# A hybrid decoder step on one core: norm factors fetched as rows from DRAM, gate products as 64x64 corners, the last token half in blocks of 228 and 114, schedule constants set anew

## The chip, the core and the metric

The kernel runs on one core of a Trainium2 chip. The metric is the device time of one execution in microseconds (us). The program is recorded through a tile layer: the code names instructions, tiles and priorities, a scheduler orders each engine's instructions once, at build time, and the chip then executes every engine's list strictly in that order, waiting on semaphores. An engine whose next instruction is not ready stands still even if a later one could run. All transfers named below are issued by SP (SyncE) or ACT, also in the order of their lists.

## What is computed

One decoder layer over 2048 prompt tokens and 8 sample tokens (2056 columns), D_MODEL 1024, all in fp32:

```python
xn = _rmsnorm(x, norm1_g)
z = jnp.einsum('btd,de->bte', xn, w_in)              # 1024 -> 1792
xr, gr, q, k, v = jnp.split(z, IN_SPLITS, axis=-1)
xc, new_conv = _causal_conv(xr, conv_buf, conv_w, conv_b)
# gates of the recurrence: 8 diagonal blocks of 64x64
r = jax.nn.sigmoid(_block_diag(xc, gate_a_w, gate_a_b))
i = jax.nn.sigmoid(_block_diag(xc, gate_x_w, gate_x_b))
...                                                   # linear recurrence -> rec
att = _prompt_attention(q, k, v, attn_sinks)          # window of 128, 8 heads
mix = jnp.concatenate([_rmsnorm(rec, rec_norm_g), _rmsnorm(att, attn_norm_g)], axis=-1)
h = x + jnp.einsum('bte,ed->btd', mix, w_out)
hn = _rmsnorm(h, norm2_g)
ff = jax.nn.silu(hn @ w_gate) * (hn @ w_up)           # 1024 -> 2816
y = h + ff @ w_down                                   # 2816 -> 1024
y_prompt = _rmsnorm(y, final_norm_g)
```

An RMSNorm multiplies each token by a factor of its own, rsqrt(mean(x²) + eps).

## The kernel before, in words

Channels lie on the 128 partitions, tokens on the free axis. Most products are split products: an operand is held as a rounded part `hi` and a remainder `lo` of type fp32r, and one product is three matmuls (hi·hi, hi·lo, lo·hi; lines L281 to L283, L1231 to L1233, L1268 to L1270, L1295 to L1297). The gate products (L608), the broadcasts (L319, L347), the sums (L304) and the transposes (L789) are plain fp32.

**First half (attention, recurrence, projections).** The tokens go in four parts s = 0 to 3 of 520, 512, 512 and 512 columns. For each part 14 units `ip` of 128 output channels each are computed (24 matmuls of 512 columns), then 8 units `op` of the output projection. A unit's weights come through a pool of five tiles; parts s > 0 fetch split weights that part 0 left in DRAM (`split_weights`, L262). The attention of part s (scores `s`, transposes `pt`, outputs `o`) and the recurrence of part s are threaded between the `ip` and `op` units of PE's list. `rec_chunk` computes the gates of 128 channels c: two 128x128 weights, each with two 64x64 blocks on the diagonal and zeros elsewhere, give two matmuls over the part's columns (four for part 0, whose 520 columns go in two halves of 260). Their results go to `m_tile`, a pool with a single PSUM bank, which the sums, the broadcasts and the transposes of V use as well; ACT reads each with a tanh (L610).

**A norm factor** is made as a column: PE sums squares over the partitions (`rstd_cols`, L304, one matmul for 86 to 128 tokens), DVE adds eps (L308), POOL takes the power −0.5 (L309). The factors of w tokens then lie on w partitions, and to multiply they must lie along the free axis on all 128. `row_bcast` (L319) does this with one fp32 matmul for each w tokens, column times identity, into `m_tile`, and ACT copies it to SBUF (L325). `half_bcast` (L347) does the same for the second norm, whose columns are kept in `rs2`.

**Second half (FFN).** The tokens go in three groups gi of two halves n (2x344, 2x342, 2x342 columns). 11 pairs p of 256 hidden channels are computed for each group: `ps_g` and `ps_u` (gate and up) and then the down product, which adds into `y`. Pairs 1 to 9 of gi = 1 and 2 use seven combined products in the place of eight (`pw`); the others use plain down products `pd`. Weights are split again for each group by ACT (hi), and by DVE or POOL (lo); tables `E_...` say for each such operation whether DVE ('V') or POOL ('P') does it.

**The end.** The last pair of gi = 2 goes half by half, n = 1 first. `finish` squares each `y` (ACT), adds the squares (POOL for n = 1, DVE for n = 0), forms the factors, and multiplies all 16 tiles (L1323, DVE), each followed by its store. Both halves are multiplied after the last product.

**What sets the order.** Each step is a generator that yields a planned time; instructions get the priority of that time, less a lead (`ahead`, the constants `L_...`, `F_...`). The scheduler takes the ready instruction with the first priority on each engine. So tables such as `T_IP`, `T_OP`, `T_ATT` and `ORDERS` decide how units, attention and recurrence lie between each other on PE, and on every other engine.

Of the kernel before, what the change touches and what calls it, by code (L numbers as in the profile page):

```python
# [12 lines left out]
P = 128  # L13
# [26 lines left out]
U_IP, U_OP = 6.19, 5.41  # L40
# [6 lines left out]
T_IP = [19.97, 89.2513, 240.41, 360.55]  # L47
T_OP = [187.9747, 327.9525, 449.0, 499.41]
T_OPA, L_LM = 524.66, 40.7
# [5 lines left out]
F_LEAD = [8.63, 18.27, 9.0, 1.0, 3.05, 1.57, 4.0, 2.24, 4.14]  # L55
F_HN = [26.25, 18.3, 31.9]
F_FIN = [13.89, 1.77, 6.51, 4.8]
F_MIX = [15.0, 62.67, 18.34, 64.97]
F_DOWN = [16.55, 11.4]
E_SUM = ['P', 'P', 'P', 'P']  # L60
E_LO0 = ['P', 'V', 'P', 'V', 'P', 'V', 'P']
E_LO1 = ['P', 'V', 'P']
E_LO2 = ['V', 'V', 'V']
E_DLO1 = ['P', 'V', 'P', 'V', 'V', 'P', 'V']
E_DLO2 = ['P', 'P', 'P', 'P', 'P', 'P', 'V']
E_DSUM = ['P', 'P', 'P', 'P', 'P', 'V', 'P', 'P']
E_T1 = ['P', 'P', 'P', 'V']
E_T2 = ['V', 'P', 'P', 'P']
E_HN = ['P', 'P', 'P', 'P']
E_MUL = ['P', 'V', 'V', 'P']  # L70

# [33 lines left out]
ORDERS = [[1, 12, 9, 8, 0, 3, 11, 10, 13, 2, 5, 4, 6, 7], [8, 9, 10, 11, 4, 0, 12, 13, 1, 5, 2, 6, 3, 7], [4, 0, 5, 1, 8, 12, 9, 10, 11, 2, 13, 7, 3, 6], [8, 12, 10, 9, 11, 13, 0, 4, 1, 6, 5, 2, 3, 7]]  # L105
T_ATT = [[-5.16, 6.82], [94.7626, 9.19], [318.03, 12.77], [454.6511, 8.38]]
T_MIX0 = 400.09
T_MIX = [None, T_B[0] + F_MIX[0], T_B[1] + F_MIX[2]]
T_REC = 46.56
L_PE, L_EV, L_DMA, L_W, L_PREP, D_PREP, L_AN, T_HN, D_HN, D_MIX = 195.07, 6.8, 44.07, 6.54, 16.82, -0.58, 33.49, 477.25, 7.78, 0.2  # L110
# [3 lines left out]
L_SW = 10.68  # L114
T_CACHE, T_LD, T_PRO = 126.26, 3.73, -37.62
D_REC = [10.95, 7.47]
D_ATT = [4.5, 3.07, 9.75, 5.73]
T_DVE = -4.47
T_DEC = 102.0
T_RN = [128.93, 254.29, 363.658, 427.88]  # L120
# [70 lines left out]
def hybrid_step(tc, xT, xR, vecs, cst, gatew, win, wout, wgate, wup, wdown, kT, vC, ck, cv, sconv, sh0,  # L191
                yT, pkT, pvT, pconv, phs, skw, svw, sconv_o, sh_o):
# [3 lines left out]
    with ExitStack() as ctx:  # L196
# [28 lines left out]

        def m_tile(name):
            return ps_m.tile([P, 512], F32, tag="m", name=name)
# [16 lines left out]
        mixed = dp.tile([3, 7, P, 4, TP], F32, name="mixed")  # L244
        split_s = {x: dp.tile([NPAIR, 4, P, 2, 512], F32, name=f"split_{x}") for x in "gu"}
# [5 lines left out]
        keep = tc.keep_in_program_order  # L251

# [25 lines left out]
        def mm3(out, ws, k, xh, xl, first, last):  # L278
            w, m0 = ws[k // 4], k % 4 * P
            wh, wl = w[:, 0, m0:m0 + P], w[:, 1, m0:m0 + P]  # L280
            nc.tensor.matmul(out, wh, xh, start=first, stop=False)  # L281
            nc.tensor.matmul(out, wh, xl, start=False, stop=False)  # L282
            nc.tensor.matmul(out, wl, xh, start=False, stop=last)  # L283
# [16 lines left out]
        def rstd_cols(acc, w, nt, which, out, name, lead=None, pin=False):  # L300
            ps = m_tile(f"st_{name}")
            with ahead(lead):
                for j in range(nt):
                    r = nc.tensor.matmul(ps[:w, j:j + 1], acc[:, j * w:(j + 1) * w], avg[:, which:which + 1],  # L304
                                         start=True, stop=True)
                    if pin and j == 0:
                        keep(r)
# [3 lines left out]
        def row_bcast(cols, w, nt, name, lead=None, keep_ps=False, pin=False):  # L311
            out = None if keep_ps else bcp.tile([P, TM], F32, tag="bc", name=f"rb_{name}")
            per = 512 // w
            for j0 in range(0, nt, per):
                jn = min(per, nt - j0)
                ps = (acc_tile if keep_ps else m_tile)(f"bc_{name}_{j0}")
                with ahead(lead):
                    for j in range(jn):
                        r = nc.tensor.matmul(ps[:, j * w:(j + 1) * w], cols[:, j0 + j:j0 + j + 1].to_broadcast([w, P]),  # L319
# [5 lines left out]
                nc.scalar.copy(out[:, j0 * w:(j0 + jn) * w], ps[:, :jn * w])  # L325
            return out
# [7 lines left out]
        def half_bcast(gi, n, name):  # L334
            o, nn = HALVES[gi][n]
            out = hbp.tile([P, TP], F32, tag="hb", name=f"hb_{name}")
            ps = m_tile(f"hb_{name}")
            for s, (c0, T, _, w, nt) in enumerate(SUBS):
                a, b = max(o, c0), min(o + nn, c0 + T)
                if a >= b:  # L340
                    continue
                j0, j1 = (a - c0) // w, (b - c0 - 1) // w + 1
                with ahead():
                    for j in range(j0, j1):
                        x, y = max(a, c0 + j * w), min(b, c0 + j * w + w)
                        d0 = x - c0 - j * w
# [1118 lines left out]
```

## Time and profile before

| | us |
|---|---|
| runs of the kernel | 2075.49, 2079.70, 2086.09 (median 2079.7) |
| profiled execution, its time | 2083.33 |
| its span, first to last instruction | 2081.6 |
| PE busy with matmuls | 2020.7 (97%) |
| DVE / ACT / POOL busy | 1438.9 / 937.7 / 935.7 |
| mean share of 16 DMA engines, queue q1 | 62.8% |

A row of a group has the line, the engine, the operation, the tiles written and read, and the count; then busy time, mean ns of one, and the idle time of the engine just before with the instruction that ended it. Matmuls overlap, so the pace of PE is read from start to start in the timeline, not from durations. One fp32 matmul that isn't a transpose shows as two records.

### The profile page before, as it was taken

Reading aid. Unit: us, or ns where it says so; the run is one execution under the profiler, and the core shown is the slowest. Engines: PE = TensorE matmul, PEld = TensorE weight load, DVE = VectorE, ACT = ScalarE, POOL = GpSimd, SP = SyncE. Lnnn points to the kernel's source line nnn. Section 1 sums busy time; section 2 is a strip of 40 time slices with the busy share of each in tenths; the row PEclk is TensorE's granted clock in tenths of the full one; section 3 lists DMA queues with packets and bytes.
Section 4 is the critical chain, followed back from the end, with each engine's and each line's share of the span. In section 5 each row is a group of like instructions: output and inputs, shape, how many; then the busy total and the mean of one; then the engine's idle time right before and its main releaser. Section 6 shows DMA issues by size and latency. Waiting matters only on the chain.

```text
span 2081.6 us, 34706 instructions
## 1 busy us (share of the span) xinstructions
PE 2020.7 (97%) x12238; PEld 1910.1 (92%) x12238; DVE 1438.9 (69%) x2683; ACT 937.7 (45%) x1954; POOL 935.7 (45%) x820
## 2 busy tenths in 40 slices
PE   8999899999999899999999999999999999999997
PEld 8988787878877799999999999999999999999997
DVE  6786885766986655656654568777776667777676
ACT  5774684553564453334334533333334533333342
POOL 5211342030123688767775845445546622332332
PEclk9999999999999899999999999999999999999998
DMA  8764485575677855556555776767677675556652
GB/s 299 258 212 155 156 290 172 186 239 191 212 265 267 290 215 195 213 194 226 197 188 178 269 263 203 246 232 236 204 249 252 235 232 197 195 189 195 196 181 94
DMA packets 208989, 450.95 MB, mean 217 GB/s; under 512 B 25232, under 2 KB 82720, under 8 KB 208800
## 3 DMA queue, kind: packets, MB, share of 16 engines
q1 hardware_dynamic: 205616, 446.24, 62.8%
q10 hardware_dynamic: 3200, 2.51, 0.4%
q8 instruction: 96, 1.57, 0.3%
q14 instruction: 77, 0.63, 0.1%
HBM read 335.89 MB, written 113.84 MB: 216 GB/s over the span
## 4 chain that ended last, share of the span: by engine, by line
PE 51%; DMA 4%; DVE 4%; POOL 3%; issue 3%; ACT 1%; SPq 0%; DVEq 0%; POOLq 0%; ACTq 0%
PE ps_u L1231 6%; PE ps_u L1232 6%; PE ps_u L1233 6%; PE ps_g L1231 5%; PE ps_g L1232 5%; PE ps_g L1233 5%; PE pw L1296 3%; PE pw L1295 3%; PE pw L1297 3%; PE pd L1268 3%; PE pd L1269 3%; PE pd L1270 3%; DMA n<-hs 2%; DVE y L1323 1%; DMA rd<-in_wdown 1%
## 5 line engine op out<-in xcount | busy, mean ns | idle before, releaser
L1231 PE MATMUL ps_g<-hn,w_g 128*128 128x342 f32 (+1 forms) x924 | 296.6, 321 | 5.5 <-DVE xres L942 2.6
L1231 PE MATMUL ps_u<-hn,w_u 128*128 128x342 f32 (+1 forms) x924 | 297.0, 321 | 1.4 <-ACT c_u L1241 0.8
L1232 PE MATMUL ps_g<-hn,w_g 128*128 128x342 f32 (+1 forms) x924 | 296.0, 320 | 2.4 <-DVE hn L433 2.4
L1232 PE MATMUL ps_u<-hn,w_u 128*128 128x342 f32 (+1 forms) x924 | 296.5, 321 | 0.0
L1233 PE MATMUL ps_g<-hn,w_g 128*128 128x342 f32 (+1 forms) x924 | 295.7, 320 | 0.0
L1233 PE MATMUL ps_u<-hn,w_u 128*128 128x342 f32 (+1 forms) x924 | 294.3, 320 | 0.0
L1301 DVE TENSOR_TENSOR y<-y,pw 128x342 f32<-128x342 f32 x504 | 238.7, 503 | 54.8 <-PE pw L1297 53.9
L281 PE MATMUL ip<-xn,w_in 128*128 128x512 f32 (+1 forms) x560 | 201.2, 364 | 8.1 <-ACT xn L286 8.1
L282 PE MATMUL ip<-xn,w_in 128*128 128x512 f32 (+1 forms) x560 | 201.8, 362 | 0.5 <-DVE xn L287 0.5
L283 PE MATMUL ip<-xn,w_in 128*128 128x512 f32 (+1 forms) x560 | 199.7, 358 | 0.0
L1231 PEld LDWEIGHTS ps_g<-hn,w_g 128*128 128x128 f32 x924 | 174.6, 189 | 7.0 <-DVE xres L942 3.0
L1231 PEld LDWEIGHTS ps_u<-hn,w_u 128*128 128x128 f32 x924 | 175.4, 190 | 2.3 <-ACT c_u L1241 1.1
L1232 PEld LDWEIGHTS ps_g<-hn,w_g 128*128 128x128 f32 x924 | 174.8, 189 | 2.7 <-DVE hn L433 2.7
L1232 PEld LDWEIGHTS ps_u<-hn,w_u 128*128 128x128 f32 x924 | 175.4, 190 | 0.0
L1233 PEld LDWEIGHTS ps_u<-hn,w_u 128*128 128x128 f32 x924 | 174.9, 190 | 0.0
L1233 PEld LDWEIGHTS ps_g<-hn,w_g 128*128 128x128 f32 x924 | 174.7, 189 | 0.0
L1272 DVE TENSOR_TENSOR y<-y,pd 128x344 f32<-128x344 f32 (+1 forms) x240 | 116.8, 506 | 75.0 <-PE pd L1270 73.4
L1197 POOL TENSOR_TENSOR c_u<-c_u,c_g 128x342 f32<-128x342 f32 (+1 forms) x60 | 63.6, 1059 | 209.4 <-DVE c_u L1215 206.3
L1269 PE MATMUL pd<-fl,w_d 128*128 128x344 f32 (+1 forms) x480 | 153.7, 320 | 0.2 <-DVE fl L1186 0.2
L1268 PE MATMUL pd<-fh,w_d 128*128 128x344 f32 (+1 forms) x480 | 151.9, 320 | 1.1 <-DVE y L1272 1.1
L1270 PE MATMUL pd<-fh,w_d 128*128 128x344 f32 (+1 forms) x480 | 152.6, 319 | 0.0
L1186 DVE TENSOR_TENSOR fl<-c_u,fh 128x342 fp32r<-128x342 f32 (+1 forms) x132 | 114.0, 870 | 54.4 <-ACT fh L1185 53.0
(308 smaller groups left out, 5299.4 us busy)
## 6 DMA issues: line engine op xcount, KB each, us to landing
w_g<-split_g SPq DMA_DIRECT2D x88, 512.0 KB, 4.3
w_u<-split_u SPq DMA_DIRECT2D x88, 512.0 KB, 5.0
w_in<-split_w SPq DMA_DIRECT2D x84, 512.0 KB, 3.3
rg<-in_wgate SPq DMA_DIRECT2D x110, 256.0 KB, 3.0
ru<-in_wup SPq DMA_DIRECT2D x110, 256.0 KB, 3.1
w_out<-split_w SPq DMA_DIRECT2D x48, 512.0 KB, 4.5
split_g<-w_g SPq DMA_DIRECT2D x44, 512.0 KB, 3.0
split_u<-w_u SPq DMA_DIRECT2D x44, 512.0 KB, 3.8
```

The costliest lines, as they stand in the source:

```text
L281: nc.tensor.matmul(out, wh, xh, start=first, stop=False)
L282: nc.tensor.matmul(out, wh, xl, start=False, stop=False)
L283: nc.tensor.matmul(out, wl, xh, start=False, stop=last)
L1186: nc.vector.tensor_tensor(lo, v, hi.bitcast(F32), ALU.subtract)
L1231: nc.tensor.matmul(ps, wh, hi, start=first, stop=False, skip_group_check=not fresh)
L1232: nc.tensor.matmul(ps, wh, lo, start=False, stop=False, skip_group_check=not fresh)
L1233: nc.tensor.matmul(ps, wl, hi, start=False, stop=kk == 3, skip_group_check=not fresh)
L1268: nc.tensor.matmul(ps, w[:, 0, c:c + P], hi, start=h == 0, stop=False)
L1269: nc.tensor.matmul(ps, w[:, 0, c:c + P], lo, start=False, stop=False)
L1270: nc.tensor.matmul(ps, w[:, 1, c:c + P], hi, start=False, stop=h == 1)
L1272: nc.vector.tensor_tensor(ys[gi, n, m], ys[gi, n, m], ps, ALU.add)
L1301: nc.vector.tensor_tensor(v, v, ps, ALU.add)
```

## The change

**Norm factors as rows.** `row_fetch` stores the column of factors to DRAM and loads it back broadcast to all partitions. It takes the place of the matmuls and the copy for the first norm of parts 1 to 3, for the recurrence group's norm of all parts, and for the final norm of gi = 0 and 1. The second norm's columns are stored to `rstd_d` as they are made, and `half_bcast` is one load. Part 0's first norm, the attention group's norm and the final norm of gi = 2 stay with matmuls.

**Gates as corners.** Each gate product is issued as 64x64 matmuls on the blocks alone: for a set of columns, two for the a gate into `m_tile` (rows 0-63 to 0-63, rows 64-127 to 64-127), and two for the x gate into a bank of `acc_tile` (three banks, shared with `ip` and `op`), crosswise (rows 0-63 to 64-127 and the other way round). The x gate's tanh becomes two instructions of 64 partitions.

**The last half in blocks.** The final down product of gi = 2, n = 0 goes in two column blocks of 228 and 114, each of all eight m. `finish_last` takes the place of `finish` there: half n = 1 gets its factors while the blocks run, six of its tiles are multiplied by ACT and POOL and two by DVE; some squares of a block are summed by PE in place of a vector add; the blocks are multiplied by DVE into contiguous tiles and leave in four larger stores to a new output `yB`.

**Constants.** Planned times, leads, unit orders and engine tables are set anew; 147 operations of the FFN's weight preparation and combinations go from POOL to DVE. `AFTER` names three places where a matmul is held behind another on PE. The core of the diff:

```diff
-U_IP, U_OP = 6.19, 5.41
+U_IP, U_OP = 6.26, 5.378
-T_IP = [19.97, 89.2513, 240.41, 360.55]
-T_OP = [187.9747, 327.9525, 449.0, 499.41]
+T_IP = [19.97, 89.18, 240.423, 359.312]
+T_OP = [173.651, 330.556, 445.257, 499.513]
+BLOCKS = [(0, 2), (2, 1)]
+AFTER = [('o9_0', 2, 'op1_5_0', 17), ('ga2_3_0', 0, 'op1_1_0', 8), ('o15_0', 0, 'op2_7_0', 16)]
...
+        def store_rows(row, cols, w, nt):
+            nc.sync.dma_start(row.rearrange("(j p) -> p j", p=w), cols[:w, :nt])
+        def load_rows(out, row, n):
+            nc.sync.dma_start(out, row.unsqueeze(0).to_broadcast([P, n]))
+        def row_fetch(cols, w, nt, name):
+            row = dp.tile([w * nt], F32, name=f"row_{name}")
+            out = bcp.tile([P, TM], F32, tag="bc", name=f"rb_{name}")
+            store_rows(row, cols, w, nt)
+            load_rows(out[:, :w * nt], row, w * nt)
+            return out
...
         def half_bcast(gi, n, name):
...
-                        nc.tensor.matmul(ps[:, x - o:y - o], rs2[:w, s, j:j + 1].to_broadcast([w, P]),
-                                         ident[:w, d0:d0 + y - x], start=True, stop=True)
-            nc.scalar.copy(out[:, :nn], ps[:, :nn])
+            load_rows(out[:, :nn], rstd_d[o:o + nn], nn)
...
-                state[s]["bc"] = row_bcast(cols[:w, :nt], w, nt, f"x{s}")
+                state[s]["bc"] = (row_fetch if s else row_bcast)(cols[:w, :nt], w, nt, f"x{s}")
...
-                for gi, (dst, hb) in enumerate(((ra, hab), (ia, hxb))):
-                    for n0, nn in nbl:
-                        ps = m_tile(f"g{s}_{c}_{gi}_{n0}")
-                            nc.tensor.matmul(ps[:, :nn], gw[:, (gi * 4 + c) * P:(gi * 4 + c + 1) * P], xc[:, n0:n0 + nn],
-                        nc.scalar.activation(dst[:, n0:n0 + nn], ps[:, :nn], AF.Tanh, bias=hb[:, c:c + 1], scale=0.5)
+                for n0, nn in nbl:
+                    pa, px = m_tile(f"ga{s}_{c}_{n0}"), gate_tile(f"gx{s}_{c}_{n0}")
+                        for r0, ps, c0 in ((0, pa, 0), (64, pa, 64), (0, px, 64), (64, px, 0)):
+                            w0 = (4 * (ps is px) + c) * P + r0
+                            mm(..., ps[c0:c0 + 64, :nn], gw[r0:r0 + 64, w0:w0 + 64], xc[r0:r0 + 64, n0:n0 + nn],
+                    nc.scalar.activation(ra[:, n0:n0 + nn], pa[:, :nn], AF.Tanh, bias=hab[:, c:c + 1], scale=0.5)
+                    for r0, c0 in ((0, 64), (64, 0)):
+                        nc.scalar.activation(ia[r0:r0 + 64, n0:n0 + nn], px[c0:c0 + 64, :nn], AF.Tanh,
...
+                if last and gi == 2:
+                    order = order[:KD] + [(m, 0, 114 * b, 114 * (b + k)) for b, k in BLOCKS for m in range(KD)]
```

How the rows of three lists move. `ga3_0` and `gx3_0` are the a and x gate of channels 0 to 127 in part 3, `ip3_1` is the input unit in which they lie. PE before:

```order
L281 MATMUL ip3_1_0_5511<-xn3_3_4576,w_in3_1_0_5439 128x512
L608 MATMUL g3_0_0_0_5605<-xc3_0_5469,gw_131 128x512
L282 MATMUL ip3_1_0_5511<-xn3_3_4576,w_in3_1_0_5439 128x512
...
L283 MATMUL ip3_1_0_5511<-xn3_6_4600,w_in3_1_1_5441 128x512
L608 MATMUL g3_0_1_0_5608<-xc3_0_5469,gw_131 128x512
L281 MATMUL ip3_1_0_5511<-xn3_7_4608,w_in3_1_1_5441 128x512
```

PE in the change, the same place:

```order
L272 MATMUL ip3_1_0_5417<-xn3_6_4626,w_in3_1_1_5345 128x512 x2
L272 MATMUL ga3_0_0_5520<-xc3_0_5373,gw_132 64x512 x2
L272 MATMUL gx3_0_0_5521<-xc3_0_5373,gw_132 64x512 x2
L272 MATMUL o12_0_6257<-pth12_0_0_6235,vt2_3_4108 128x512
L272 MATMUL ip3_1_0_5417<-xn3_7_4634,w_in3_1_1_5345 128x512 x3
```

The two gates stood 22 rows apart, since both used the one bank of `m_tile`; here their four corners follow each other. Elsewhere other rows stand between the a and the x corners: in part 1, channels 256 to 383, the change has

```order
L272 MATMUL op0_0_260_3050<-mix0_1_2234,w_out0_0_0_2942 128x260
L272 MATMUL ga1_2_0_3083<-xc1_2_2934,gw_132 64x512 x2
L272 MATMUL op0_0_260_3050<-mix0_1_2234,w_out0_0_0_2942 128x260 x2
L272 MATMUL op0_0_260_3050<-mix0_2_2455,w_out0_0_0_2942 128x260 x3
L272 MATMUL op0_0_260_3050<-mix0_3_2462,w_out0_0_0_2942 128x260 x3
L272 MATMUL op0_0_260_3050<-mix0_4_2593,w_out0_0_1_2948 128x260 x3
L272 MATMUL op0_0_260_3050<-mix0_5_2601,w_out0_0_1_2948 128x260
L272 MATMUL gx1_2_0_3084<-xc1_2_2934,gw_132 64x512 x2
```

so that PE goes from 128-wide to 64-wide products twice. Over the whole list the corners stand in 33 such stretches; in seven of them an a pair and an x pair are adjacent, five of 512 and two of 260 columns.

POOL at the end of the program, in the change (`cols_f2_0_0` and `cols_f2_0_1` are the factors of the two blocks, `y2_m` tiles of half n = 1):

```order
L1435 TENSOR_TENSOR y2_0_18240<-y2_0_18240,bs_f2_1_2_22490 128x342
L1435 TENSOR_TENSOR y2_1_18249<-y2_1_18249,bs_f2_1_2_22490 128x342
L1419 TENSOR_TENSOR cols_f2_0_0_22572<-cols_f2_0_0_22572,nhalf_108 114x2
L1435 TENSOR_TENSOR y2_1_18249<-y2_1_18249,bs_f2_1_2_22490 128x342
L1419 TENSOR_TENSOR cols_f2_0_1_22616<-cols_f2_0_1_22616,nhalf_108 114x1
L1435 TENSOR_TENSOR y2_2_18267<-y2_2_18267,bs_f2_1_2_22490 128x342
L1435 TENSOR_TENSOR y2_3_18286<-y2_3_18286,bs_f2_1_2_22490 128x342 x2
```

Before, the last two rows of POOL's list were the two powers of the factors (L309), with nothing between them. Here three multiplications stand ahead of the last power and three behind it.

SP's list in the change, around the fetch of the recurrence norm's factors of part 3 (`row_rc3` is the store, `rb_rc3` the load; `w_out2_7` are weights of the last `op` unit of part 2):

```order
L470 DMA m0_1_0_6125<-mixed_112 128x344
L367 DMA row_rc3_6188<-rccols3_6180 128x4x1
L300 DMA w_out2_7_0_6384<-split_w_117 128x1024
L470 DMA m0_1_1_6134<-mixed_112 128x344
L370 DMA rb_rc3_6189<-row_rc3_6188 128x512
L939 DMA hs_111<-xres2_4_6071 128x512
L300 DMA w_out2_7_1_6386<-split_w_117 128x1024
```

Before, neither row was there: the broadcast was four matmuls on PE between `op2_7` and `op3_0`, and the sums for it stood in `op2_7`; they now stand in `op2_4`, three units earlier.

More of the change, by code (lines that the diff above doesn't have):

```diff
@@ L251, in hybrid_step, with mm, tr, behind @@
         keep = tc.keep_in_program_order
+        issued = {}
+        def mm(key, *args, **kw):
+            r = nc.tensor.matmul(*args, **kw)
+            issued.setdefault(key, []).append(r)
+            return r
+        def tr(key, *args):
+            r = nc.tensor.transpose(*args)
+            issued.setdefault(key, []).append(r)
+            return r
+        no_sync = mybir.DependencyInfo(mybir.DependencyClass.NoSync, mybir.DependencyReason.DATA)
+        def behind(later, earlier):
+            tc.add_manual_dep(later.ins, earlier.ins.name, no_sync, reason="issue order")
+        def order_pe():
+            for later, i, earlier, j in AFTER:
+                if later in issued and earlier in issued:
+                    behind(issued[later][i], issued[earlier][j])
         def col(i):
@@ L276, in split_weights, with mm3 @@
             return ws
-        def mm3(out, ws, k, xh, xl, first, last):
+        def mm3(key, out, ws, k, xh, xl, first, last):
             w, m0 = ws[k // 4], k % 4 * P
             wh, wl = w[:, 0, m0:m0 + P], w[:, 1, m0:m0 + P]
-            nc.tensor.matmul(out, wh, xh, start=first, stop=False)
-            nc.tensor.matmul(out, wh, xl, start=False, stop=False)
-            nc.tensor.matmul(out, wl, xh, start=False, stop=last)
+            mm(key, out, wh, xh, start=first, stop=False)
+            mm(key, out, wh, xl, start=False, stop=False)
+            mm(key, out, wl, xh, start=False, stop=last)
         def split(hi, lo, src, g):
@@ L303, in rstd_cols @@
                 for j in range(nt):
[L304 removed]
+                    r = mm(f"st_{name}", ps[:w, j:j + 1], acc[:, j * w:(j + 1) * w], avg[:, which:which + 1],
                                          start=True, stop=True)
@@ L1363, in hybrid_step @@
             ch.run()
+            order_pe()
 _INS = [
```

241 lines of the change are left out of this document (164 added, 77 removed).

## The prediction, as put on record before the run

> **What bounds the kernel now.** I read the page first: the span, the busy row and the chain that ended last; then busy time by stage, then the waits of PE.
>
> ```profile
> span 2081.6 us, 34706 instructions
> PE 2020.7 (97%) x12238; PEld 1910.1 (92%) x12238; DVE 1438.9 (69%) x2683; ACT 937.7 (45%) x1954; POOL 935.7 (45%) x820
> ...
> PE 51%; DMA 4%; DVE 4%; POOL 3%; issue 3%; ACT 1%; SPq 0%; DVEq 0%; POOLq 0%; ACTq 0%
> ```
>
> PE is busy for 97% and leads the chain; the next engine, DVE, has 69%. So what counts is how many products PE issues, at what pace, and where it stands still. In the table by stage the columns are the window, its us, busy time of PE, weight loads, DVE, ACT and POOL, the granted clock, the DMA share and GB/s:
>
> ```profile
> 0.00:725.00 725.00, 686.51 (x3761) 582.84 (x3762) 536.60 (x1127) 411.70 (x873) 212.80 (x215) 0.97 0.67 228
> 725.00:2050.00 1325.00, 1314.13 (x8354) 1308.19 (x8353) 881.18 (x1513) 517.21 (x1063) 714.66 (x597) 1.00 0.63 214
> ```
>
> The first half of the layer (to 725) leaves PE idle for 725 − 686.5 = 38.5 us at a clock of 0.97; the FFN (to 2050) leaves 10.9 in 1325 us at a clock of 1.00. So only the first half has much to give back in waits. They are named in the view of PE's waits (us in total, times, longest):
>
> ```profile
> PE ip L281 <- ACT xn L286: 8.1, 1, 8.1
> PE g L608 <- ACT ra L610: 5.8, 3, 3.8
> PE pw L1295 <- DVE y L1301: 4.9, 7, 1.0
> PE o L800 <- DVE ratt L805: 3.9, 5, 1.9
> ...
> PE st_at L304 <- ACT ia L610: 2.6, 1, 2.6
> ...
> PE o L800 <- ACT pth L792: 2.3, 2, 1.6
> ...
> PE o L801 <- DVE ptl L793: 1.3, 3, 0.6
> ```
>
> The 8.1 us are the start, which the change leaves alone. `g` and `st_at` wait for a tanh to read the one bank of `m_tile`: 8.4 us. Attention outputs `o` wait for DVE and ACT: 7.5 us. A wait costs more than its length, as the timeline shows behind the longest (start, duration, wait in brackets):
>
> ```profile
> 270.60 1.12 PE L608 MATMUL g<-xc,gw 128*128 128x512 f32 x2 [3.84 <-ACT ra L610]
> ...
> 272.06 0.42 PE L281 MATMUL op<-mix,w_out 128*128 128x260 f32 x1
> 272.27 0.42 PE L282 MATMUL op<-mix,w_out 128*128 128x260 f32 x1
> ```
>
> After it, 260 columns take 0.21 us from start to start; 512 take 0.24 at full pace (rows below), so 260 should take 0.12. The clock is granted lower behind a wait. Over the first half that is 725 × (1 − 0.97) = 22 us.
>
> **The change: broadcasts that go.** The groups of the broadcast matmuls, with counts by shape:
>
> ```profile
> L319 PE MATMUL bc_x<-cs,xcols x34: 253/275/417, 30.9 to 445.4; 128*128 128x128 f32 x24, 104*128 104x104 f32 x10
> L319 PE MATMUL bc_rc<-cs,rccols x34: 255/275/356, 209.4 to 636.7; 128*128 128x128 f32 x24, 104*128 104x104 f32 x10
> L319 PE MATMUL bc_f<-cs,cols_f x40: 238/275/423, 1200.3 to 2071.4; 114*128 114x114 f32 x24, 86*128 86x86 f32 x16
> L347 PE MATMUL hb<-cs,rs x44: 167/275/356, 487.5 to 1180.1; 128*128 128x128 f32 x16, 104*128 104x104 f32 x8, 104*128 104x32 f32 x2, 104*128 104x72 f32 x2
> ```
>
> Part 0's ten `bc_x` stay, and the last group's twelve `bc_f`: 24 + 34 + 28 + 44 = 130 records go. Their pace, from six of them and the next instruction:
>
> ```profile
> 301.54 0.83 PE L319 MATMUL bc_x<-cs,xcols 128*128 128x128 f32 x6
> 302.21 0.27 PE L789 MATMUL pt<-cs,sc 128*128 128x128 f32 x1
> ```
>
> That is 0.67 / 6 = 0.11 us each, so 130 × 0.11 = **−14 us**, all on PE's path. In their place SP gets 15 small stores and 17 loads. No transfer of this form stands in the trace; the nearest are larger ones (KB each, median us from issue to landing):
>
> ```profile
> mixed<-n SPq DMA_DIRECT2D x56, 171.0 KB, 2.1
> n<-hs SPq DMA_DIRECT2D x32, 171.0 KB, 4.0
> w_in<-split_w SPq DMA_DIRECT2D x84, 512.0 KB, 3.3
> ```
>
> A store and then a load are 2.1 + 4.0 = 6.1 us, where matmuls and copy took about 1.5. What covers it: the rows of SP's list show the fetch for part 3's recurrence with its sums three output units earlier, and a unit is 24 × 0.24 = 5.7 us, so 17 us stand against 6. Behind the load, which waits for its store, SP holds weights of the next units; five tiles are 5 × 2.8 us (half a unit each) = 14 us of stock against 6.1 + 3.3. I take 0; where the cover is gone each of the 17 fetches can hold PE for up to 6 us, and a few would.
>
> **Gates as corners.** The price of a gate now, between two `ip` matmuls of 512 columns:
>
> ```profile
> 528.25 1.02 PE L608 MATMUL g<-xc,gw 128*128 128x512 f32 x2
> 528.71 0.80 PE L282 MATMUL ip<-xn,w_in 128*128 128x512 f32 x1
> 529.34 0.40 PE L283 MATMUL ip<-xn,w_in 128*128 128x512 f32 x1
> ```
>
> From 528.25 to 529.34 less one `ip` (0.24) is 0.85 us for a gate of 512 columns; by columns 0.43 for one of 260. Before, there are 24 of the first and 16 of the second. What corners of the array cost beside full products, the trace shows only where small matmuls of 64 rows and 64 columns stand among `ip`:
>
> ```profile
> 172.02 0.40 PE L283 MATMUL ip<-xn,w_in 128*128 128x512 f32 x1
> 172.26 0.39 PE L281 MATMUL ip<-xn,w_in 128*128 128x512 f32 x1
> 172.58 0.27 PE L854 MATMUL dS<-cs,dw 64*128 64x64 f32 x1
> ...
> 173.21 0.43 PE L855 MATMUL dS<-dw,ones 64*128 64x64 f32 x2
> ...
> 173.90 0.39 PE L281 MATMUL ip<-xn,w_in 128*128 128x512 f32 x1
> ```
>
> From 172.26 to 173.90 PE did three `ip` (0.72) and three small records (0.33, at the broadcasts' 0.11): 0.6 us are over for two entries into the 64-wide form, 0.3 each. The order shows 33 such stretches: 33 × 0.3 = +9.9. If two corners with different rows and columns run side by side, an a pair takes the slot of one gate and nothing is won; only the seven places with a and x adjacent could put four corners in one slot and save 5 × 0.85 + 2 × 0.43 = 5.1. I take both: 9.9 − 5.1 = **+5 us**. Bounds: all gates at half price and free entries, −14; corners one after the other, each of 40 pairs a slot longer, 24 × 0.85 + 16 × 0.43 = 27, with the entries +37. Of the two I stand nearer the first, as the `dS` rows are small matmuls with a price per entry and no more.
>
> The Trainium skill, "TensorEngine Tiling (Array Packing)", section "Key Properties", says that a change of tiling mode drains TensorE; it speaks against this order with its 33 stretches, and the 0.6 us of the `dS` rows agree. By "TensorE: Matmul & The Clock Gate", section "Part 3: Packing small matmuls", tiles packed together end about one span after the first starts plus some 4 ns each; by it alone the term would be −5 in place of +5. No row here shows two at once.
>
> **Waits.** x gates now go to the three banks shared with `ip` and `op`, so a gate no longer waits for the other's tanh: the 8.4 us go, −8. `AFTER` holds `o9_0` and `o15_0`, two outputs that waited, behind later matmuls, and attention of part 3 comes two to three units earlier: I take half of the 7.5 us of `o`, −4. If these waits go, a third of the 22 us of low clock goes too, −7. With −1 for broadcasts that shared the bank: **−20 us**. What is late next: a gx tile holds one of three banks until ACT has read it twice.
>
> ```profile
> L610 ACT ACTIVATE ra<-g,hab 128x512 f32<-128x512 f32 x12 | 8.1, 678 | 4.1 <-PE g L608 4.1
> ```
>
> Three tanh of 0.68 are 2 us, and the other two banks cover two units, 11 us. Behind a held `ip` matmul all of PE's list waits, so ACT's queue has to be 9 us late before that costs. Bounds: −50 (of 38.5 − 8.1 + 22 all but a few us) to +10 (new waits as long as the old ones that go).
>
> **FFN engines.** 147 operations move from POOL to DVE. The same operation on each (busy us, mean ns):
>
> ```profile
> L1099 POOL TENSOR_TENSOR wd<-rd,wd 128x512 fp32r<-128x512 f32 x72 | 98.7, 1371 | 78.1 <-ACT wd L1098 75.3 <-DMA rd<-sums_d 2.8
> L1099 DVE TENSOR_TENSOR wd<-rd,wd 128x512 fp32r<-128x512 f32 x27 | 23.6, 875 | 0.2 <-ACT wd L1098 0.2
> ```
>
> 147 × 0.875 = 129 us more on DVE, from 881 to 1010 of 1325 (76%). Both engines stay under PE, and PE stands only 10.9 us there, 4.9 of it on DVE's `y`. These waits can shrink (POOL's slow ones go) or grow (DVE's queue): I take 0, bounds −8 and +10.
>
> **The end.** Last down product and what follows, on PE, DVE and POOL:
>
> ```profile
> 2066.29 0.33 PE L1270 MATMUL pd<-fh,w_d 128*128 128x342 f32 x1
> 2066.45 0.67 PE L304 MATMUL st_f<-avg,acc_f 128*114 128x1 f32 x6
> ...
> 2069.98 7.79 DVE L1323 SCALAR_TENSOR_TENSOR y<-y,vec,bc_f 128x342 f32<-128x342 f32 x16 [0.60 <-PE bc_f L319]
> ```
>
> ```profile
> 2069.21 0.16 DVE L308 TENSOR_SCALAR cols_f<-st_f 114x3 f32<-114x3 f32 x1 [0.91 <-PE st_f L304]
> ```
>
> ```profile
> 2055.05 6.97 POOL L298 TENSOR_TENSOR acc_f<-acc_f,sq_f 128x342 f32<-128x342 f32 x7 [8.52 <-ACT sq_f L297]
> ```
>
> Now PE ends its products at 2066.45, the factors take 3.5 us (to 2069.98), DVE 7.8, the last store 3.8 (to 2081.6): 15.1. In the change 48 matmuls of 342 columns at 0.16 (7.5 us) become 96 that cannot go under the 0.11 of a small record (10.6): +3.1. Twenty records of sums and broadcasts now stand ahead of the last product: +2.2. Factors as before, 3.5. DVE multiplies sixteen narrower tiles: 0.16 fixed (its row with 3 columns) and (0.49 − 0.16) / 342 for a column give 0.38 for 228 and 0.27 for 114, 8 × 0.65 = 5.2 (bounds 3.9, by columns alone, and 7.8). Then 3.8. Together 17.8 in place of 15.1, +2.7. POOL's list has a multiplication of 1.0 us ahead of the last power, which may add some: **+3 us** (−3 to +8).
>
> **The rivals.** *Waits go, corners are cheap:* two thirds of the 60 us of idle and slow clock go (−40), and entries cost nothing beside them: −14 + 0 − 40 + 3 = −51, **2029**. For it: the order is moved just where PE stood; against: the 7.5 us of `o` depend on DVE and ACT, not on the bank.
>
> *Waits change place:* the list is strict, and a gate or an `o` put elsewhere waits for another tanh or DVE's queue: −14 + 5 + 0 + 3 = −6, **2074**, within 0.5% of before.
>
> *Slower, corners one after the other:* if an a pair takes two slots, PE works 27 us longer besides the 9.9 of entries, and the longer gates eat half of the waits' gain: −14 + 37 − 10 + 3 = +16, **2096**. With the waits' gain halved, the corners decide against the change from 14 + 10 − 3 = 21 us; less the 9.9 of entries and shared by 40 pairs that is 0.28 us for a pair over a gate of before. For it: no row shows two corners at once, and both corners of a pair write one bank. By the same skill page on tiling, section "Gotcha 1: PSUM Pressure", different row tiles cannot access one PSUM bank at the same time; that rule would give this rival. Against: the `dS` rows bear no price beyond the entry, though they lie in one corner.
>
> That the change doesn't do what it says is not open: the order's rows show broadcasts gone, corners adjacent at seven places, and sums three units earlier.
>
> **How the numbers follow.** −14 + 5 − 20 + 3 = −26 on the profiled execution's 2083.3: 2057. The median of the runs, 2079.7, lies 3.6 below that execution, so the forecast is **2054**, chance 0.40 (own range 2040 to 2068). The rivals get 0.27, 0.17 and 0.16. The range runs from 2022, a little under the second case, to 2088, which takes in the third and leaves out most of the last. About 0.5% is what a measurement of this kernel can tell from no change: faster is under 2069, slower over 2090, hence 0.67, 0.17 and 0.16.
>
> **What would show it.** Right: no `g` wait on a tanh; first-half idle under 25 us at a clock of 0.98; a stretch of four 512-column corners at most 0.3 us longer than before's single gate; 12.5 us from the last `pd` to the end; FFN idle still about 11. Wrong: corners of a pair with starts 0.4 us apart each; `xn`, `mix` or `hn` waiting for a row load; `ip` or `op` waiting for a bank that a gx tile holds; `ps_g` and `pw` waiting on DVE for more than 20 us in sum.

## The result, and the profile after

The changed kernel took 2170.7 us (median of 4 runs, 2167.5 to 2178.2) beside 2079.4 for before: ratio 1.0441, 95% interval 1.0401 to 1.048. It is slower by 83 to 100 us, where 25 us faster was forecast. The profiled execution took 2167.5 us. Its page begins:

```profile
span 2165.3 us, 34766 instructions
## 1 busy us (share of the span) xinstructions
PE 2035.9 (94%) x12246; PEld 1901.5 (88%) x12246; DVE 1485.5 (69%) x2841; ACT 954.2 (44%) x1971; POOL 775.0 (36%) x683
...
PE 62%; DMA 18%; DVE 10%; ACT 3%; issue 3%; POOL 3%; SPq 1%; DVEq 0%; POOLq 0%; ACTq 0%
```

PE's busy time has hardly changed (+15 us), but DMAs went from 4% to 18% of the chain that ended last, and DVE from 4% to 10%. By stage the tables of both kernels are cut at the first product of the FFN (at 692.1 before, 758.4 now) and at the last product (first before, then after; columns as above):

```profile
0.00:692.10 692.10, 660.98 (x3640) 558.72 (x3641) 513.24 (x1099) 395.31 (x840) 190.89 (x201) 0.98 0.66 224
692.10:2066.40 1374.30, 1356.06 (x8575) 1348.15 (x8574) 915.99 (x1564) 541.52 (x1113) 743.07 (x618) 1.00 0.63 213
2066.40:2081.60 15.20, 3.70 (x26) 3.19 (x24) 9.72 (x22) 0.90 (x2) 1.71 (x2) 0.64 0.53 184
```

```profile
0.00:758.40 758.40, 671.54 (x3633) 545.98 (x3633) 516.28 (x1098) 405.65 (x848) 184.51 (x199) 0.95 0.66 207
758.40:2153.40 1395.00, 1362.33 (x8601) 1353.83 (x8599) 963.86 (x1726) 548.09 (x1122) 585.80 (x480) 0.99 0.63 212
2153.40:2165.30 11.90, 2.07 (x16) 1.67 (x15) 5.37 (x18) 0.47 (x2) 4.65 (x6) 0.65 0.60 222
```

The first half is 66.3 us longer, and PE's idle time there went from 31.1 to 86.9 us; the clock fell from 0.98 to 0.95. The second stage is 20.7 us longer, the last 3.3 shorter. The waits of PE are new ones, and all but one of the longest end with DVE:

```profile
PE s L272 <- DVE mx L814: 12.2, 3, 10.7
PE pt L277 <- DVE ptl L836: 10.6, 3, 6.3
PE pd L272 <- DVE y L1322: 10.4, 3, 4.6
PE gx L272 <- DVE xr L611: 10.1, 1, 10.1
PE ps_g L272 <- DVE c_u L1241: 8.5, 2, 4.5
PE ip L272 <- ACT w_in L309: 8.4, 1, 8.4
PE ip L272 <- DVE kraw L611: 8.2, 1, 8.2
```

What DVE stands at, from the view of its waits:

```profile
DVE rrec L717 <- DMA rb_rc<-row_rc: 34.3, 4, 14.7
DVE y L1371 <- DMA rb_f<-row_f: 28.0, 4, 8.5
...
DVE kraw L611 <- DMA rb_x<-row_x: 11.4, 1, 11.4
...
DVE n L415 <- DMA hb<-rstd_d: 8.7, 1, 8.7
```

These are 82 us at row loads. One of them, the recurrence norm's fetch of part 1, can be followed through three timelines, SP, DVE and PE:

```profile
343.85 0.38 SPq L367 DMA_DIRECT2D row_rc<-rccols  x1
354.92 0.32 SPq L370 DMA_DIRECT2D rb_rc<-row_rc  x1
355.34 1.58 SPq L300 DMA_DIRECT2D w_in<-split_w  x3
```

```profile
359.82 0.75 DVE L717 SCALAR_TENSOR_TENSOR rrec<-rrec,vec,rb_rc 128x512 f32<-128x512 f32 x1 [14.73 <-DMA rb_rc<-row_rc]
```

```profile
350.77 2.33 PE L272 MATMUL ip<-xn,w_in 128*128 128x512 f32 x9
363.22 1.12 PE L272 MATMUL gx<-xc,gw 64*64 64x512 f32 x2 [10.11 <-DVE xr L611]
```

The store is issued at 343.85; SP stands for 11 us until it has landed and issues nothing else, three weight loads among them; the load lands after another 4.9; DVE has stood 14.7 us (from 345.1), and PE 10.1, since the eviction of `xr` stands behind DVE's held multiplication.

### The profile page after: what moved, and what is told of

It is laid out like the page before. It is cut to its first block, busy times and chain, and to the rows that moved or that the text cites. A ratio compares the mean times of both kernels' runs of the same rounds, so it can differ in the third digit from the quotient of the medians.

```text
span 2165.3 us, 34766 instructions
## 1 busy us (share of the span) xinstructions
PE 2035.9 (94%) x12246; PEld 1901.5 (88%) x12246; DVE 1485.5 (69%) x2841; ACT 954.2 (44%) x1971; POOL 775.0 (36%) x683
## 2 busy tenths in 40 slices
DMA packets 218067, 454.58 MB, mean 210 GB/s; under 512 B 32646, under 2 KB 90646, under 8 KB 217878
## 4 chain that ended last, share of the span: by engine, by line
PE 62%; DMA 18%; DVE 10%; ACT 3%; issue 3%; POOL 3%; SPq 1%; DVEq 0%; POOLq 0%; ACTq 0%
PE ps_u L272 17%; PE ps_g L272 16%; PE pw L272 10%; PE pd L272 8%; PE ip L272 7%; DMA n<-hs 2%; PE op L272 2%; DMA row_rc<-rccols 1%; DMA xt<-in_xR 1%; DMA rd<-in_wdown 1%; DMA m<-mixed 1%; DMA row_x<-xcols 1%; DMA mixed<-n 1%; DMA rstd_d<-rs 1%; DVE sc L825 1%
## 5 line engine op out<-in xcount | busy, mean ns | idle before, releaser
L272 PE MATMUL ps_g<-hn,w_g 128*128 128x342 f32 (+1 forms) x2772 | 498.9, 324 | 14.7 <-DVE c_u L1241 8.5
L272 PE MATMUL ps_u<-hn,w_u 128*128 128x342 f32 (+1 forms) x2772 | 484.1, 320 | 2.9 <-DMA w_u<-split_u 1.4
L272 PE MATMUL ip<-xn,w_in 128*128 128x512 f32 (+1 forms) x1680 | 353.2, 361 | 18.4 <-ACT w_in L309 8.4
L272 PEld LDWEIGHTS ip<-xn,w_in 128*128 128x128 f32 x1680 | 274.7, 194 | 71.2 <-issue 11.6
L272 PE MATMUL pd<-fh,w_d 128*128 128x344 f32 (+3 forms) x992 | 244.4, 319 | 10.4 <-DVE y L1322 10.4
L272 PE MATMUL op<-mix,w_out 128*128 128x512 f32 (+1 forms) x960 | 200.3, 361 | 9.2 <-DMA w_out<-split_w 7.0
L272 PEld LDWEIGHTS op<-mix,w_out 128*128 128x128 f32 x960 | 159.5, 194 | 42.0 <-issue 8.4
L272 PEld LDWEIGHTS pd<-fh,w_d 128*128 128x128 f32 x992 | 173.9, 190 | 11.6 <-DVE y L1322 11.3
L272 PE MATMUL pw<-fh,wd 128*128 128x342 f32 x576 | 167.4, 320 | 3.0 <-DVE y L1351 3.0
L272 PE MATMUL pd<-fl,w_d 128*128 128x344 f32 (+3 forms) x496 | 158.3, 319 | 0.0
```

Source lines behind the costliest of these rows:

```text
L272: r = nc.tensor.matmul(*args, **kw)
```

## The experiments

Theories: **A**, DVE stands at the row loads and PE behind it; **S**, SP's list, standing at each load, holds back other transfers; **D**, the 4-byte packets of the stores slow other transfers (D1 on their queue, D2 on all); **B**, the new constants and order lose the time; **C**, gx tiles hold the banks of the units; **R**, any edit makes the scheduler lay a new list, and the times were set for the old one. Ratios are to the kernel before, measured beside each.

**No fetch.** e1_bcast:

```diff
-state[s]["bc"] = (row_fetch if s else row_bcast)(...)
+state[s]["bc"] = row_bcast(...)        # the same for rc, f; half_bcast by matmuls
```

> The changed kernel with all 17 row loads and 15 row stores taken back: every norm factor is spread by matmuls on PE and an ACT copy, as before the change; corners, blocks and constants stay. Theory A (DVE stands at the row loads, PE behind it, and that is nearly the whole loss): DVE's 82 us of waits on row loads go, 130 records (14 us) come back, so 2062 to 2090 us. Theory B (the new order and constants lose the time, wherever the factors come from): 2140 to 2180 us. Theory C (corners and gx banks): 2140 or more as well, with waits at ga and gx kept.

2144.9 us, ratio 1.0295 (1.0271 to 1.0319). Theory A as the whole cause fell: 61 us of loss remain with no fetch at all. In the trace nearly all of it lies in the first half: the first product of the FFN starts at 752.0 us in place of 692.1, with PE idle for 69.0 us in place of 31.1 and the clock at 0.96 in place of 0.98. The second stage is only 4.5 us longer than before, so of its 20.7 us in the change 16 came with the fetches.

**The fetch, for nobody.** e2_idle_fetch has in addition every store and load, into a scratch; e11_idle_store the stores alone; e15_idle_store_pool the same stores issued by GpSimd. PE's list in the first two is the same, instruction for instruction, as in e1_bcast; in the third 3 of 12104 stand elsewhere. DVE's and ACT's lists are the same but for at most three places.

```diff
+bc = row_bcast(...); store_rows(row, cols, w, nt)      # e11
+load_rows(scratch[:, :w * nt], row, w * nt)            # e2 too
-nc.sync.dma_start(row.rearrange("(j p) -> p j", p=w), cols[:w, :nt])
+nc.gpsimd.dma_start(row.rearrange("(j p) -> p j", p=w), cols[:w, :nt])   # e15
```

> As the first kernel, all factors spread by PE, but the 15 row stores are issued as well and each row is loaded 128-fold into a DRAM scratch that nobody reads: the traffic and SP's queue without the wait on DVE. Theory A: within 15 us of the first kernel, 2062 to 2100 us, and row stores still take about 11 us to land. Theory D (the 4-byte packets of the row stores and the loads slow the weights on the queue, and that is the loss): 2130 us or more.

> As the second kernel, but only the 15 row stores are issued and no load: SP never stands behind a store, and nobody reads the rows. Theory S (the 62 us that idle fetches cost over no fetches come from SP's list standing at each load): 2135 to 2160, as with no fetch (2145). Theory D (the 4-byte packets of the stores hold up the other transfers): 2175 us or more. If the loads' own 128-fold reads are what costs: also 2135 to 2160, and then SP's standing and the loads stay one.

> As the kernel with idle stores (2181), but the 15 stores are issued by GpSimd on its own queue, right behind the powers that GpSimd itself makes. PE's list is the same but for 3 of 12104 instructions. Theory D1 (SP's queue: what is issued behind a store lands late): 2143 to 2158, as without stores (2145). Theory D2 (4-byte stores hold up the DMA engines whatever the queue): 2170 us or more.

| | us | over e1_bcast |
|---|---|---|
| e2_idle_fetch | 2206.6 (ratio 1.0592, 1.0561 to 1.0623) | +62 |
| e11_idle_store | 2180.9 (1.0466, 1.0436 to 1.0497) | +36 |
| e15_idle_store_pool | 2170.7 (1.0428, 1.0398 to 1.0458) | +26 |

With one list on PE, fifteen stores of 2 KB that nobody waits for cost 36 us, on another queue still 26; the loads cost 26 more. So D holds, mostly in the form D2. The view of `w_in` tells how: first over the whole of e1_bcast, then in e15_idle_store_pool between 355 and 365 us, with a store issued at 358.94 on GpSimd's queue (time from issue to landing):

```profile
DMA to landing us min/median/max: 3.1/3.6/5.9
```

```profile
DMA to landing us min/median/max: 9.1/11.4/12.3
```

Weights on SP's queue that are issued around a store on GpSimd's land after 9 to 12 us in place of 3.6. It isn't this one place: over the whole of e15_idle_store_pool, 26 transfers whose landing can be read were issued while such a store was on its way, and took 9.1 us in the median; the other 694 took 3.7. The stores themselves (KB each, us to landing), e15_idle_store_pool:

```profile
row_x<-xcols POOLq DMA_DIRECT2D x3, 2.0 KB, 10.4
row_rc<-rccols POOLq DMA_DIRECT2D x3, 2.0 KB, 11.1
rstd_d<-rs POOLq DMA_DIRECT2D x3, 2.0 KB, 10.0
```

S: in e2_idle_fetch SP stands at the loads, for stores to land:

```profile
SPq L370 <- DMA row_rc<-rccols: 38.1, 4, 11.9
...
SPq L370 <- DMA row_f<-cols_f: 33.6, 4, 9.7
...
SPq L370 <- DMA rstd_d<-rs: 30.6, 4, 8.6
...
SPq L370 <- DMA row_x<-xcols: 15.8, 2, 8.0
```

118 us of standing go with 26 us of loss. The loads' own traffic isn't told apart from SP's standing.

**Whole rows.** e3_row_store, the changed kernel with the factors transposed first; e12_before_row_store and e4_before_fetch put the two kinds of fetch into the kernel before:

```diff
+nc.tensor.transpose(ps[:nt, :w], cols[:w, :nt], ident[:w, :w])
+nc.scalar.copy(rows[:nt, :w], ps[:nt, :w])
-nc.sync.dma_start(row.rearrange("(j p) -> p j", p=w), cols[:w, :nt])
+nc.sync.dma_start(row.rearrange("(j p) -> j p", p=w), rows[:nt, :w])
```

> The changed kernel, but the factors are first transposed by PE to nt rows of w factors, copied by ACT, and stored as rows of 416 or 512 bytes in place of single factors of 4 bytes; the loads are as in the changed kernel. Theory A with the 4-byte store as its size (11 us of the 15.7 us of a round trip): a store takes about 2 to 3 us, DVE's waits on row loads fall from 82 to 20 us or less, time 2090 to 2135 us. If a store's time is that of the queue and not of its packets: stores still about 10 us and 2155 us or more.

> The kernel before with the row stores and loads alone, at the same places and for the same norms as in the change; gates, end and constants of before. Theory A: DVE waits of 60 to 100 us on row loads, 2130 to 2170 us. Theory B and C: about 2066 (the 14 us of matmuls go) to 2085 us.

> The kernel before with fetches alone, the factors stored as whole rows after a transpose on PE. The kernel before with 4-byte stores took 2204. Theory D+S (4-byte stores hold up SP's queue, loads stand behind them): most of the 121 us goes, 2080 to 2125 us, where the 14 us of matmuls gained stand against a new list (23 us in the control). If a fetch costs as such, by its wait at the load: 2150 or more.

e3_row_store 2118.1 (ratio 1.0166, 1.0139 to 1.0193), 53 us under the changed kernel; e4_before_fetch 2204.5 (1.0595, 1.056 to 1.0631), far over what theory A said; e12_before_row_store 2103.8 (1.0101, 1.0069 to 1.0134), some 100 us less with the same norms fetched. What SP waits for stores in e3_row_store, and DVE for row loads:

```profile
SPq L374 <- DMA rstd_d<-hr: 6.4, 3, 2.5
...
SPq L374 <- DMA row_rc<-rb_rc: 5.2, 3, 2.6
...
SPq L374 <- DMA row_x<-rb_x: 1.7, 2, 1.2
...
SPq L374 <- DMA row_f<-rb_f: 0.4, 1, 0.4
```

```profile
DVE y L1375 <- DMA rb_f<-row_f: 10.5, 3, 5.3
...
DVE xr L615 <- DMA rb_x<-row_x: 4.2, 1, 4.2
...
DVE rrec L721 <- DMA rb_rc<-row_rc: 3.4, 4, 1.5
DVE n L419 <- DMA hb<-rstd_d: 3.3, 1, 3.3
...
DVE kraw L615 <- DMA rb_x<-row_x: 1.2, 1, 1.2
```

SP's standing falls from the 87 us of the changed kernel to 14, DVE's from 82 to 23. The row's form, 4 bytes or some 500, is what made the fetch dear; the list is also a new one in both, so the 53 and 100 us aren't the stores' price alone. With cheap fetches e3_row_store is also 27 us under e1_bcast, which has the same gates, end and constants and spreads the factors by matmuls. The Trainium skill, "DMA: Bandwidth & Descriptors", section "Rules for kernel authors", says that a pattern whose last dimension isn't contiguous becomes one descriptor for each element, and advises to rearrange it. The runs bear it out: the packets under 512 bytes fall from 32646 in the changed kernel to 25524 here, by about as many as factors are stored (7020), and the load of the fetch followed above, issued 11.1 us behind its store there, is issued 2.0 us behind it here.

**Loads from GpSimd.** e7_load_pool:

```diff
-nc.sync.dma_start(out, row.unsqueeze(0).to_broadcast([P, n]))
+nc.gpsimd.dma_start(out, row.unsqueeze(0).to_broadcast([P, n]))
```

> The changed kernel with the row loads issued from GpSimd's list in place of SP's; the stores stay on SP. So SP no longer stands behind a load that waits for its store, but DVE still needs the row as late. Theory A1 (DVE stands at the multiplication, PE behind it): 2150 us or more, since the round trip stays at 15 us. Theory A2 (SP's list standing 87 us holds back weights and tiles, and that is most of what the fetch costs): 2100 to 2135 us.

2201.6 (ratio 1.0571, 1.0554 to 1.0587), far over the range of theory A2. DVE's waits at the rows grow to 91 us, and GpSimd stands 126 us. Standing only moves to another engine; some 500 of PE's 12246 records moved too, so the size says little.

**Corners and banks.** e5_before_corners puts the corner gates into the kernel before; e9_corners_m the corners but both gates in `m_tile`; e10_x_bank full gates but x in an acc bank.

```diff
-ps = m_tile(f"g{s}_{c}_{gi}_{n0}")
+ps = (acc_tile if gi else m_tile)(f"g{s}_{c}_{gi}_{n0}")     # e10
-nc.tensor.matmul(ps[:, :nn], gw[:, g0:g0 + P], xc[:, n0:n0 + nn], ...)
+for r0 in (0, 64):                                           # e9
+    nc.tensor.matmul(ps[r0:r0 + 64, :nn], gw[r0:r0 + 64, w0:w0 + 64], xc[r0:r0 + 64, n0:n0 + nn], ...)
```

> The kernel before with the corner gates alone (x gates into the three acc banks, x tanh in two halves). PE's list then has 26 stretches of corners, 12 of them with a and x adjacent. From the changed kernel's trace a lone pair of 512 costs 0.36 us more than a full gate and an adjacent four 0.48 us less than two, so the products come out even (+0.4 us). Theory B (constants) and A (fetches): the bank waits of g (6 us) and their slow clock go, 2068 to 2084 us. Theory C (gx tiles hold acc banks, units wait): 2100 us or more.

> The kernel before with each gate as two corners, but both gates in the one bank of m_tile as before, one gate at a time, one tanh each. 40 lone pairs at 0.36 us over a full gate are +14 us, so 2094 to 2100 if the corners cost only their entries. Theory C (gx tiles in the acc banks lose the 42 us of corners alone): 2092 to 2102. Theory R (any edit makes the scheduler lay a new list, whose waits are worse than those of the list that the times were chosen for): 2105 to 2135.

> The kernel before with full gates, the x gate's result in one of the three acc banks: the bank alone, no corners. Theory C: 2110 to 2130, units waiting for banks that ACT has not read. Theory R: 2100 to 2125, with the waits spread over attention and gates. If neither bank nor list costs and the m_tile waits go: 2068 to 2080.

2125.7 (1.0196, 1.0179 to 1.0213), 2111.0 (1.0131, 1.0095 to 1.0167) and 2115.2 (1.0149, 1.0122 to 1.0177). The first and the last are not what products or banks give: the waits of a unit for a gx bank (`ip` for ACT's `ia`) are 1.7 us in e5_before_corners and 2.4 in e10_x_bank. The rest is spread over attention and gates. In e9_corners_m 40 lone pairs at 0.34 us over a full gate (below) make 14 of its 28 us.

**Constants.** e6_consts is the kernel before with the changed constants, e8_old_consts the change with the old ones.

> The kernel before with the changed constants alone (times, leads, orders, engine tables): no fetch, no corners, old end, no AFTER. Theory B (these constants lose the 60 us that the first kernel of the experiments kept without fetches): 2115 to 2150 us. If the constants are harmless by themselves and the loss came from corners or the end: 2070 to 2090 us.

> The changed kernel with the constants of before (all that exist there) and without AFTER: fetches, corners and blocks stay. If the changed constants lose 40 to 60 us: 2105 to 2130 us. If they go with the fetches and gain or do nothing there: 2165 to 2210 us, as the kernel before with fetches alone (2204).

2101.2 (1.0088, 1.0069 to 1.0107) and 2234.0 (1.0738, 1.0704 to 1.0773). The new constants lose 18 us in the old program, and with `AFTER` gain 63 in the new one: each set fits its own program better. Both times lie outside the ranges that were stated.

**Controls: a new list and nothing else.**

```diff
-T_OP = [187.9747, ...          # e13
+T_OP = [189.5, ...
-T_REC = 46.56                  # e16
+T_REC = 50.0
```

> A control: the kernel before with one planned time moved, the start of part 0's output units from 187.97 to 189.5 us. The instructions are the same ones; 605 of PE's 12011 and 246 of DVE's 2683 stand elsewhere in their lists. Theory R: 2095 to 2125 us from this alone. If a new list is harmless: 2075 to 2090 us.

> Second control: the kernel before with one planned time of the recurrence moved from 46.56 to 50.0 us; the same instructions, 384 of PE's 12011 and 170 of DVE's 2683 elsewhere in their lists. Theory R: 2090 to 2115 us, less than the first control (605 moved, +23 us) or like it. If that control was an odd one: 2076 to 2088 us.

2106.7 (1.0111, 1.0081 to 1.0141) and 2097.5 (1.0071, 1.004 to 1.0102): 23 and 15 us for the same instructions in another order. So a new list can cost that much by itself; two controls do not tell what an arbitrary one costs. The waits of PE in e13_t_op, in which attention's `o` went from 3.9 to 10.0:

```profile
PE o L800 <- DVE ratt L805: 10.0, 6, 3.3
...
PE g L608 <- ACT ra L610: 4.0, 5, 1.0
PE bc_at L319 <- POOL atcols L309: 4.0, 2, 2.6
PE ip L281 <- DVE rrec L572: 4.0, 1, 4.0
```

**What is left.** e14_rows_full_gates is e3_row_store with the full gates of before. e20_blocks and e19_rowf change one thing each in a list that stays as it was until then: the new end alone, and the final norm of gi = 0 and 1 fetched in whole rows.

> The changed kernel with whole-row stores (2118) and with the full gates of before in place of the corners. If corners cost the 28 to 42 us that they cost alone: 2078 to 2095 us. If that cost was the new list and not the corners: 2105 to 2130 us, as the list is new again.

> The kernel before with the new end alone: last half in blocks of 228 and 114, finish_last, four larger stores. PE's, DVE's and SP's lists are otherwise the same, with nothing moved. The prediction's term is +3 us (-3 to +8), so 2082 to 2087 beside 2082; from the changed kernel's trace, where 12.0 us follow the last product in place of 15.1 and the products and sums before it take 5 us more, +2. If the sums done early and the four stores gain what they are for: 2074 to 2079 us.

> The kernel before with the fetch of the final norm of the first two groups alone (four fetches), stored as whole rows. PE's list is unchanged up to the FFN's second group; 28 broadcast records go (3 us), four small transposes come. If fetches with whole rows are harmless where the list around them stays: 2077 to 2084 us. If DVE's wait for the row (10.5 us in the changed kernel with whole rows) reaches PE: 2088 to 2095 us.

e14_rows_full_gates 2108.9 (1.0125, 1.0098 to 1.0152): 9 us under e3_row_store, in a list that is new again. Full gates did not bring back the 28 to 42 us that corners cost when put in alone. e20_blocks 2083.2 beside 2082.1 (1.0002, 0.9988 to 1.0015): the end is worth −2.5 to +3 us. e19_rowf 2086.3 (1.0029, 1.0014 to 1.0044): four fetches in whole rows cost 3 to 9 us though 3 us of matmuls went. That lies between the two ranges stated, and some 370 other records of PE moved in the FFN, so it isn't the fetches' price alone. No kernel of these beat the one before.

## Why the prediction was wrong

Two steps failed: the fetch at nothing, and the waits at −20 us. By time the second is the larger, since e1_bcast, without any fetch, keeps 61 of the 91 us.

**The fetch, "I take 0"**, rests on "A store and then a load are 2.1 + 4.0 = 6.1 us". The 2.1 came from a transfer of 171 KB in rows; a store of 512 single factors has another form, and that was known from the diff. It landed after 11.0 us, the load after 4.9 more: 16 in place of 6. The price in the bounds, "each of the 17 fetches can hold PE for up to 6 us", was too low for the same reason. SP's standing was in it as 6.1 + 3.3 against a stock of 14 us; with 16 in place of 6.1 the stock no longer covers it, SP stands 87 us in all, and `op` waits 7.0 us for weights. One way of paying wasn't in it at all: other transfers land 5 to 9 us late. With PE's list unchanged the fetches cost 62 us even when nobody uses them. Against the 14 us of matmuls that they save, the changed kernel is 26 us over e1_bcast; its constants suit its program, as e8_old_consts shows.

**The cover** was argued for one fetch, the recurrence norm's of part 3, from PE's list (sums three units earlier, 17 us). There DVE stands only 1.5 us at the row, which landed 15.5 us behind the store's issue; but that is no proof of the cover, since DVE came late itself. For a load of `m`, issued 0.5 us ahead of the store, ACT waited until 11.2 us after its issue, and DVE, behind ACT, stood 8.5 us. The cover was taken over to nearly all of the 17 fetches, and at the same row of parts 0, 1 and 2 DVE stands 5.6, 14.7 and 12.5 us. In part 1 DVE reached its multiplication right after SP had issued the store (345.1 and 343.9 us). PE's list doesn't tell that; the question should have been, fetch by fetch, what stands ahead of the multiplication in DVE's list.

**Waits, −20 us.** The mechanism was right in the small: `g` no longer waits for ACT's tanh (5.8 us before; 0.3 for `gx` now). But the term took the rest of the list to be as good as before, and its other parts have the wrong sign: "half of the 7.5 us of `o`" and "a third of the 22 us of low clock" were to go. In e1_bcast, where no fetch disturbs, `o` waits some 25 us in all, 16.2 of them here:

```profile
PE o L271 <- DVE ratt L859: 16.2, 9, 4.6
```

Its first half has 38 us more of idle time, and the lower clock (0.96 in place of 0.98) makes up most of the rest of the 60. So what failed is the step from moved rows to vanished waits: the order was changed where PE had stood, and PE now stands at other rows. The parts alone give 18 (constants), 41 (corners) and 0 (end); that their sum, 59, is near 61 proves little, since each was measured in a list of its own. The controls show that 15 to 23 us of such a loss can come from a new list alone. How much of the 41 is that and how much a lasting price of corners and banks stays open.

**Gates, +5 us.** Right in mechanism, near in size. A lone pair in a row of `ip`, then four side by side (PE of the changed kernel):

```profile
410.93 0.85 PE L272 MATMUL ip<-xn,w_in 128*128 128x512 f32 x3
411.71 1.08 PE L272 MATMUL gx<-xc,gw 64*64 64x512 f32 x4
412.71 1.44 PE L272 MATMUL ip<-xn,w_in 128*128 128x512 f32 x5
```

```profile
372.69 0.86 PE L272 MATMUL ip<-xn,w_in 128*128 128x512 f32 x3
373.72 0.65 PE L272 MATMUL ga<-xc,gw 64*64 64x512 f32 x2 [0.17 <-DVE xc L634]
373.74 0.65 PE L272 MATMUL gx<-xc,gw 64*64 64x512 f32 x2
374.17 0.62 PE L272 MATMUL ga<-xc,gw 64*64 64x512 f32 x2
374.21 0.60 PE L272 MATMUL gx<-xc,gw 64*64 64x512 f32 x2
374.74 1.43 PE L272 MATMUL ip<-xn,w_in 128*128 128x512 f32 x5
```

From 410.93 to 412.71, less three `ip` (0.72), the pair takes 1.06 us; from 372.69 to 374.74, less `ip` and the wait, all four take 1.16, with a and x started 0.02 us apart. So corners run side by side. The first `ip` behind them is slow too: in single records, which the rows above merge, the next one starts 0.34 us after it in place of 0.23. The prediction priced the full gate up to the second matmul behind it; measured to that point, with 0.23 for each `ip`, a pair takes 1.20, four take 1.28 and a full gate 0.86. For 260 columns these are 0.78, 0.78 and 0.44. So an entry costs 0.34, and the 33 stretches come to 33 × 0.34 − 5 × 0.86 − 2 × 0.44 = +6 us. The rival "corners one after the other" had the sign of the result by a mechanism that isn't there. The Trainium skill, "TensorEngine Tiling (Array Packing)", section "Gotcha 1: PSUM Pressure", on which it leaned, differs from this trace: the two corners of a pair have different rows, write one bank, and share a slot.

**Broadcasts, −14 us**, are not measured alone; 130 records went from PE's list. The 27 us between e3_row_store and e1_bcast have the sign that was forecast, but the two lists differ. **FFN engines, 0:** in e6_consts, with the new tables, the time from the first FFN product to the end is 1392 us (713 to 2105) in place of 1389 (692 to 2082): right. **The end, +3 us:** 12.0 us follow the last product (12.5 forecast), and e20_blocks has it within −2.5 to +3. The range failed because it took the fetch's bound from the wrong rows and gave the new list no price.

## What to carry to other kernels

Price a DMA by the form of its rows, not by its bytes: here 1.3 to 2 KB in 4-byte pieces took 6 to 11 us and made transfers near it as late, and a transpose ahead of it brought the time down to about 2. Ask of a fetch which engine's list holds its reader, and which list holds the load, before calling it covered. In a kernel whose order was set for one program, give a new order a price too (15 and 23 us, about 1%, in the two controls here), and make a control that moves the order alone before blaming the edit.

## What the runs showed of the hardware that was not expected

A store of 342 to 520 single fp32 values took 9 to 13 us to land from GpSimd's queue (medians of its groups in e15_idle_store_pool); from SP's, in the changed kernel, the load that waits for it was issued 6 to 11 us behind it. Weight loads on another queue issued near a store took 9 to 12 us in place of 3.6. Fifteen such stores in some 2150 us cost 26 to 36 us of the kernel's time with nobody waiting for them. Row loads of 256 KB, 128 times the same 2 KB, landed in 4.5 to 4.7 us in the changed kernel. Four corners of 64x64 with 512 columns took 1.28 us and two alone 1.20, beside 0.86 for one full 128x128 gate.
